# Probability times values in groups B and C: P's transpose as the stationary operand, values streaming

## The chip, the cores and the metric

The kernel runs on one core of a Trainium2 chip. The metric is device microseconds of one execution; less is better. The engines are TensorE (PE in the profile; its weight loads stand apart as PEld), VectorE (DVE), ScalarE (ACT), GpSimd (POOL) and the DMA queues that SyncE (SP), ACT and POOL issue to. In a matmul one operand, the stationary one, is first loaded into the array (a weight load), then the other, the moving one, streams through it; the result lands in PSUM. In this kernel a product of float32 operands shows two weight loads and two matmul records in the trace, one pair per pass; a product of the rounded type float32r shows one.

## The reference

Two layers, each a mixer of four parallel head groups over 2048 latent tokens and 256 context tokens (2304 keys, 18 tiles of 128). A is grouped-query attention, D a state-space scan; neither is touched. B and C matter here:

```
# B, per head: two softmax maps over all 2304 keys, then one product with the values
p1 = softmax32(einsum('bhqd,bhtd->bhqt', q1, k1) * scale)
p2 = softmax32(einsum('bhqd,bhtd->bhqt', q2, k2) * scale)
o  = einsum('bhqt,bhtd->bhqd', p1 - lam * p2, v)      # d = 64
y  = rms_norm(o, subln_g) * (1 - lam_init)
# C, per head: 8x16 clamped neighbourhood on a 64-wide grid, plus all 256 context keys
p  = softmax32(concat([s_win + bias, s_ctx]))
o  = einsum('bhwij,bhiwjd->bhwd', p_win, v_win) + einsum('bhwt,bhtd->bhwd', p_ctx, vc)
```

Each group has 4 heads of 64 channels. Context queries (2 tiles) are computed in the first layer alone. Every output is multiplied by its gate; concatenation, output projection and layer norm follow.

## The kernel before

A layer runs D and the first projection, then a chain of ten attention units (`a0, b0, a1, b1, c0, b2, c1, b3, c2, c3`), then the output projection. A unit b or c is one head: `attend` walks over query tiles of 128 (16 latent, 2 more for context in layer 0). Within the chain the order of the instructions on PE, ACT and DVE is the order in which the code is written; outside it a scheduler orders them. Into the unit that runs, `F` (a queue of "fill" work, the next unit's projection) puts matmul triples at fixed places (`F.pe()`, lines 377 to 379, tile `pj`), with their ACT and DVE steps.

One iteration `i` of `attend` works on several query tiles at once: scores of tile i+1, softmax of tile i, transposes, copies and value products of tiles i-1 and i-2, norm or finish of tile i-2 or i-3.

- `scores` (L1001): float32r matmuls into the PSUM banks `sx`, `sy`, `sz`. `maxes` (DVE L1045, or L1039 and L1041 in C) and `exp` (ACT L1060, into SBUF tiles `Ta`, `Tb`) follow. B's second map is folded in by `combine` (DVE L1084).
- `trans` (L1100): PE transposes P by key tile of 128, four at a time, into `tr`; `evac` (ACT L1114) copies the four to SBUF as `PT` (keys on the partitions, queries along the row).
- `pv` (L1126): one product per key tile. The stationary operand is the tile of values (keys x 64 channels), the moving one `PT` (keys x 128 queries). Even key tiles write partitions 0 to 63 of `acc`, odd ones 64 to 127; so the output is channels by queries, in two partial sums, and each product uses half of the array's columns.
- `ycopy` (L1131, ACT) copies `acc` to SBUF as `ys`; `ysum` (L1137, PE) multiplies it, as stationary operand, with `fold` (two identities of 64, one below the other): this adds the halves and turns the sum to queries by channels, in a new `acc`.
- `norm` (B: ACT L1143 and L1147, two POOL steps) and `finish` (DVE L1156) read that `acc`, scale, gate, and a DMA writes the output.

B has 18 key tiles per latent query tile: four groups of 4 and one of 2. C has, for the 12 interior query tiles of a head, 7: two context tiles and four full ones, and last a half tile of 64 keys, so that this product has 64 rows; the 4 edge tiles have 6. Context queries have 2. `acc` is one PSUM bank with one buffer.

The trace names the values by the tile that holds them in the unit (`b_v`, `a_q`, `a_gt`).

Of the kernel before, what the change touches and what calls it, by code (L numbers as in the profile page):

```python
# [9 lines left out]
F32 = mybir.dt.float32  # L10
# [148 lines left out]
class Net:  # L159
# [10 lines left out]
    def consts(self):  # L170
        nc, io = self.nc, self.io
        c = self.c = self.pool(self.es, "consts")
        self.dram = self.pool(self.es, "scratch", space=bass.MemoryType.DRAM)
        self.psum = self.pool(self.es, "psum", space=bass.MemoryType.PSUM)
        jp = c.tile([128, 128], I32, name="jp")
        nc.gpsimd.iota(jp, pattern=[[1, 128]], base=0, channel_multiplier=-1)
        self.ident = c.tile([128, 128], F32, name="ident")
        nc.vector.tensor_scalar(self.ident, jp, 0.0, None, op0=OP.is_equal)
        self.mhalf = c.tile([128, 8], F32, name="mhalf")
        nc.vector.memset(self.mhalf, -0.5)  # L180
        self.one = c.tile([128, 1], F32, name="one")
        nc.vector.memset(self.one, 1.0)
        self.fold = c.tile([128, 128], F32, name="fold")
        for i in range(2):
            nc.vector.tensor_add(self.fold[:, i * 64:i * 64 + 64], self.ident[:, 0:64], self.ident[:, 64:128])
        self.half = c.tile([128, 64], F32, name="half")
        nc.vector.memset(self.half, 0.5)
        self.two = c.tile([128, 128], F32, name="two")
        nc.vector.memset(self.two, 2.0)
        self.mod = [c.tile([128, 24, 2], F32, name=f"mod{l}") for l in range(DEPTH)]  # L190
        self.bT = [c.tile([128, 24], F32, name=f"bT{l}") for l in range(DEPTH)]
        for l in range(DEPTH):
            nc.sync.dma_start(self.bT[l], io["b_ada_t"][l])
        self.coef = [c.tile([128, 2, 2, 16], F32, name=f"coef{l}") for l in range(DEPTH)]
        self.cs = c.tile([128, NK, 2], F32, name="cs")
        cc = c.tile([128, NK, 2], F32, name="cc")
        nc.sync.dma_start(cc, io["cc"])
        th = c.tile([128, NK, 2], F32, name="th")
        nc.scalar.activation(th, cc, AF.Tanh, scale=0.5)
        nc.vector.scalar_tensor_tensor(self.cs, th, 1.0, cc, op0=OP.add, op1=OP.mult)  # L200
        nc.vector.tensor_scalar(self.cs, self.cs, 0.5, None, op0=OP.mult)
        dr = self.dram
        self.hs = {(l, t): dr.tile([128, 2, NK, 128], F32, name=f"hs{l}_{t}") for l in range(DEPTH) for t in range(NT)}
        self.x1 = {t: dr.tile([128, D], F32, name=f"x1_{t}") for t in range(NT)}
        self.dg = {t: dr.tile([128, 256], F32, name=f"dg_{t}") for t in range(NT)}
        self.y = {(l, t): dr.tile([128, D], F32, name=f"y{l}_{t}")
                  for l in range(DEPTH) for t in range(NT if l == 0 else NLAT)}
# [746 lines left out]
    def attend(self, l, G, F):  # L954
# [161 lines left out]
        def pv(t, g):  # L1116
            grp, g0, nkt = group(t, g)
            if not grp:
                return
            if g == 0:  # L1120
                acc[t] = self.ps_acc(128)
            PT = R[t, 0].pop(("PT", g))
            for j, (kt, c, w) in enumerate(grp):
                x = g0 + j
                half = 0 if x == nkt - 1 and nkt % 2 else x % 2
                nc.tensor.matmul(acc[t][half * 64:half * 64 + 64, :], G["v"][:w, kt, :], PT[:w, j, :], start=(x < 2),  # L1126
                                 stop=x >= nkt - 2)

        def ycopy(t):
            ys = R[t, 0]["ys"] = p.tile([128, 128], F32, name="ys")  # L1130
            nc.scalar.activation(ys, acc.pop(t), AF.Copy)  # L1131

        def ysum(t):

            r = R[t, 0]
            y = self.ps_acc(128)
            nc.tensor.matmul(y, r["ys"], self.fold, start=True, stop=True)  # L1137
            r["y"] = y[:, 0:64]

        def norm(t):  # L1140
            r = R[t, 0]
# [17 lines left out]
        def at(i, f, *a):  # L1159
            if 0 <= i < n:  # L1160
                f(steps[i], *a)
# [19 lines left out]
        for i in range(n + (3 if maps == 2 else 2)):  # L1181
            if maps == 2:
                at(i - 2, pv, 1)
                F.act()
                at(i, maxes, 0)
                at(i, neg_max, 0)
                at(i - 1, sums, 1)
                at(i - 1, recip, 1)
                at(i - 1, factor)
                at(i, exp, 0, 0)  # L1190
                at(i, scores, 1, 0)
                at(i - 1, combine, 0)
                at(i, exp, 0, 1)
                F.pe(1)
                at(i, scores, 1, 1)
                F.pe(1)
                if not early:
                    at(i - 2, trans, 2)
                at(i - 2, evac, 2)
                at(i - 2, trans, 3)  # L1200
                at(i, exp, 0, 2)
                at(i - 2, evac, 3)
                at(i, scores, 1, 2)
                at(i - 2, pv, 2)
                at(i - 2, trans, 4)
                F.dve()
                F.pe(1)
                at(i - 3, finish)
                at(i, maxes, 1)
                at(i - 2, pv, 3)  # L1210
                F.act()
                F.pe(1)
                F.pe()
                F.act()
                early = i < n and not F.merged
                at(i - 2, evac, 4)
                F.act()
                if early:
                    at(i - 1, trans, 0)
                at(i - 2, pv, 4)  # L1220
                yield half()
                at(i, sums, 0)
                at(i, neg_max, 1)
                at(i, recip, 0)
                at(i, exp, 1, 0)
                at(i, exp, 1, 1)
                if not early:
                    at(i - 1, trans, 0)
                at(i + 1, scores, 0, 0)
                F.pe()  # L1230
                at(i - 1, evac, 0)
                F.act()
                at(i + 1, scores, 0, 1)
                at(i - 1, trans, 1)
                at(i - 1, combine, 1)
                at(i - 2, ycopy)
                at(i, exp, 1, 2)
                at(i - 2, ysum)
                at(i - 1, evac, 1)
                at(i + 1, scores, 0, 2)  # L1240
                prep_at(i + 4, prep_q)
                F.pe(1)
                at(i - 2, norm)
                if i % 2:
                    F.keys()
                F.act()
                prep_at(i + 2)
                F.pe(2)
                if i % 2 == 0:
                    F.keys(1)  # L1250
                    F.keys_copy()
                F.keys_copy()
                at(i - 1, pv, 0)
                early = i + 1 < n and not F.merged
                F.dve()
                if early:
                    at(i - 1, trans, 2)
            else:
                if i == 0:
                    at(0, maxes, 0)  # L1260
                    at(0, neg_max, 0)
                    at(1, scores, 0)
                F.pe()
                at(i + 1, maxes, 0)
                at(i - 1, trans, 0)
                at(i - 1, trans, 1)
                at(i, exp, 0, 0)
                at(i - 2, ycopy)
                at(i - 1, sums, 0)
                at(i - 2, ysum)  # L1270
                at(i, exp, 0, 1)
                at(i - 1, evac, 0)
                F.pe(2)
                F.dve()
                at(i - 1, evac, 1)
                prep_at(i + 3)
                F.act()
                F.pe(1)
                at(i - 1, recip, 0)
                at(i + 1, neg_max, 0)  # L1280
                yield half()
                at(i - 2, finish)
                F.pe(1)
                prep_at(i + 5, prep_q)
                F.pe()
                F.pe(2)
                F.pe(1)
                at(i + 2, scores, 0)
                F.keys()
                F.act()  # L1290
                at(i - 1, pv, 0)
                F.dve()
                at(i - 1, pv, 1)
                F.pe(1)
                F.act()
                F.keys_copy()
            half()
            yield i < n - 1
# [705 lines left out]
```

## Time and profile before

| | |
|---|---|
| three runs | 5153.1, 5156.62 (median), 5166.4 us |
| profiled execution | 5158.76 us, its span 5156.9 us |
| mean granted TensorE clock | 0.958 of 2.4 GHz |
| PE busy | 91% of the span |
| ACT busy, DVE busy | 50%, 62% |
| units b and c | 803 to 1034, 1321 to 1530, 1550 to 2230, 3384 to 3620, 3900 to 4940 us |

A PE record begins when the instruction is issued and ends when its last result has left the array, so records of matmuls that follow each other overlap; the time that one costs the engine is the distance between starts, or between ends, in a steady row of them. A record that waits for its weights begins early and is long. The shapes in a PE record are rows by columns of the stationary operand, joined by `*`, and then those of the moving one. `<- issue` behind idle time means that the profile shows no other instruction that was waited for.

### The profile page before, as it was taken

The page shows a single profiled execution, that of the slowest core. Times are in us where ns is not written, and L with a number is a line of the kernel's source. Part 1 is how long each engine was busy: PE and PEld are TensorE (multiplying, and loading weights), DVE is VectorE, ACT ScalarE, POOL GpSimd, SP SyncE. Part 2 cuts the span into 40 slices and gives each one's busy share as a digit, 9 for nine tenths or more (in the row PEclk, how much of TensorE's full clock was granted, in tenths as well). Part 3 has the DMA queues.
Part 4 walks back from the last instruction along what each step waited for, and adds up shares of the span by engine and source line. Part 5 has one row for each costly group of instructions (what it writes and reads, how often), then busy time and mean ns, then how long its engine had stood idle before and what let it go on. Part 6 is the DMA issues. An engine that isn't in the chain of part 4 may idle for free. (4 is left out here: it accounts for less than half of the span.)

```text
span 5156.9 us, 85866 instructions
## 1 busy us (share of the span) xinstructions
PE 4681.1 (91%) x31076; PEld 3585.3 (70%) x31076; DVE 3215.5 (62%) x7061; ACT 2568.4 (50%) x6522; POOL 1912.5 (37%) x3035
## 2 busy tenths in 40 slices
PE   7788998899999999998996879988999999999998
PEld 3686646665678777776676866566657777877777
DVE  8473767676674846724972737686767648476245
ACT  3332346634675856744341233466346658566431
POOL 4363443434233233321642534434342332333112
PEclk8899999999999999999998999999999999999999
DMA  7847212322235344253668573123223343433432
GB/s 255 287 151 202 88 41 66 98 95 72 91 121 167 103 144 132 83 178 116 194 213 281 169 198 109 49 65 98 95 72 98 111 152 100 155 122 117 130 134 107
DMA packets 360184, 677.66 MB, mean 131 GB/s; under 512 B 161872, under 2 KB 262224, under 8 KB 306768
## 3 DMA queue, kind: packets, MB, share of 16 engines
q0 software_dynamic: 54432, 396.39, 22.9%
q1 hardware_dynamic: 299280, 270.47, 17.9%
q10 hardware_dynamic: 6048, 5.31, 0.3%
q8 instruction: 247, 4.05, 0.3%
q14 instruction: 177, 1.45, 0.1%
HBM read 561.66 MB, written 110.36 MB: 130 GB/s over the span
## 5 line engine op out<-in xcount | busy, mean ns | idle before, releaser
L377 PE MATMUL pj<-WH,hs 128*128 128x256 f32 (+2 forms) x2592 | 814.9, 314 | 22.1 <-ACT b_v L733 7.1
L378 PE MATMUL pj<-WL,hs 128*128 128x256 f32 (+2 forms) x2592 | 753.3, 291 | 2.7 <-POOL WL L367 2.7
L379 PE MATMUL pj<-WH,hs 128*128 128x256 f32 (+2 forms) x2592 | 752.3, 290 | 0.0
L1114 ACT ACTIVATE PT<-tr 128x512 f32<-128x512 f32 (+1 forms) x788 | 440.5, 559 | 310.0 <-PE tr L1100 303.3
L377 PEld LDWEIGHTS pj<-WH,hs 128*128 128x128 f32 x2592 | 498.1, 192 | 125.3 <-issue 68.2
L388 POOL DMA_DIRECT2D hs<-hs x378 | 227.7, 603 | 956.0 <-PE pj L379 475.6
L378 PEld LDWEIGHTS pj<-WL,hs 128*128 128x128 f32 x2592 | 499.2, 193 | 26.6 <-POOL WL L367 3.3
L881 ACT ACTIVATE PT<-sx 128x512 f32<-128x512 f32 x584 | 315.3, 592 | 378.1 <-PE sx L879 367.6
L379 PEld LDWEIGHTS pj<-WH,hs 128*128 128x128 f32 x2592 | 497.7, 192 | 2.4 <-issue 2.4
L1045 DVE TENSOR_REDUCE sm<-sx 128x1 f32<-128x1024 f32 (+1 forms) x276 | 321.8, 1166 | 210.2 <-PE sx L1001 208.9
L1060 ACT ACTIVATE Ta<-sx,sm 128x1024 f32<-128x1024 f32 (+1 forms) x340 | 324.5, 955 | 108.2 <-DVE sm L1054 87.2
L886 PE MATMUL acc<-PT,a_v 128*64 128x512 f32 (+1 forms) x1168 | 315.8, 617 | 0.0
L897 POOL TENSOR_TENSOR Ta<-Ta,PT 128x512 f32<-128x512 f32 x160 | 219.5, 1389 | 204.4 <-ACT PT L881 203.9
L1126 PE MATMUL acc<-PT,b_v 128*64 128x128 f32 (+1 forms) x3200 | 277.9, 290 | 4.4 <-DVE sm L1073 1.5
L1001 PE MATMUL sx<-b_kst,qs 128*128 128x512 f32 (+2 forms) x618 | 218.3, 441 | 58.1 <-ACT Ta L1060 57.4
L814 DVE TENSOR_REDUCE mxa<-sy 128x1 f32<-128x1024 f32 (+1 forms) x256 | 209.8, 820 | 89.9 <-PE sy L812 86.8
L897 DVE TENSOR_TENSOR Ta<-Ta,PT 128x512 f32<-128x512 f32 x288 | 217.0, 794 | 77.0 <-ACT PT L881 76.5
L878 PE MATMUL sx<-Tb,a_kst 128*128 128x512 f32 x584 | 246.8, 423 | 19.5 <-ACT PT L881 19.5
L1100 PE MATMUL tr<-ident,Ta 128*128 128x128 f32 x1576 | 246.5, 278 | 13.9 <-ACT PT L1114 10.2
L1045 DVE TENSOR_REDUCE sm<-sy 128x1 f32<-128x768 f32 (+1 forms) x260 | 245.4, 944 | 15.7 <-PE sy L1001 14.4
L814 DVE TENSOR_REDUCE mxa<-sz 128x1 f32<-128x512 f32 x256 | 175.5, 686 | 123.5 <-PE sz L812 121.7
L377 PE MATMUL s<-WH,hs 128*128 128x256 f32 (+1 forms) x576 | 193.4, 337 | 44.9 <-DMA hs<-hs 20.7
(388 smaller groups left out, 12175.2 us busy)
## 6 DMA issues: line engine op xcount, KB each, us to landing
hs<-hs POOLq DMA_DIRECT2D x378, 1024.0 KB, 5.2
hs<-hs SPq DMA_DIRECT2D x36, 1024.0 KB, 4.8
hs<-in_w_ada SPq DMA_DIRECT2D x48, 512.0 KB, 4.5
wst<-in_w_in SPq DMA_DIRECT2D x576, 32.0 KB, 1.9
yin<-y SPq DMA_DIRECT2D x30, 512.0 KB, 4.0
h<-in_xT SPq DMA_DIRECT2D x18, 512.0 KB, 6.6
U<-ud SPq DMA_DIRECT2D x64, 144.0 KB, 3.6
x<-zn SPq DMA_DIRECT2D x18, 512.0 KB, 2.7
```

Of the source, the lines that this page charges most:

```text
L377: nc.tensor.matmul(ps, H[:, k, :], WH[k][:, c0:c1], start=(k == 0), stop=False)
L378: nc.tensor.matmul(ps, H[:, k, :], WL[k][:, c0:c1], start=False, stop=False)
L379: nc.tensor.matmul(ps, L[:, k, :], WH[k][:, c0:c1], start=False, stop=(k == NK - 1))
L814: nc.vector.tensor_reduce(nm if one else mx[:, j:j + 1], s, axis=AX.X, op=OP.max, negate=one)
L878: nc.tensor.matmul(o[:, h * 512:h * 512 + w], kst[:, ks], Q[0][:, h, :w], start=True, stop=False)
L881: nc.scalar.activation(PTs[x][h][:, :w], o[:, h * 512:h * 512 + w], AF.Exp, scale=0.125)
L886: nc.tensor.matmul(acc[h * 64:(h + 1) * 64, :w], v[:, kts[x], :], PT[h][:, :w], start=(x == 0), stop=(x == n - 1))
L897: eng.tensor_tensor(sums[e][:, h, :w], first[:, :w], PT[h][:, :w], op=OP.add)
L1045: nc.vector.tensor_reduce(mx[:, j:j + 1] if len(tiles) > 1 else nm, s, axis=AX.X, op=OP.max, negate=len(tiles) == 1)
L1060: nc.scalar.activation(r["P"](a, b), src, AF.Exp, bias=r["sm"][:, 5:6], accum_out=r["sm"][:, 6 + j:7 + j])
L1114: nc.scalar.activation(PT[:w, x:y], tr[:w, x * 128:y * 128].rearrange("p (a b) -> p a b", b=128), AF.Copy)
L1126: nc.tensor.matmul(acc[t][half * 64:half * 64 + 64, :], G["v"][:w, kt, :], PT[:w, j, :], start=(x < 2), stop=x >= nkt - 2)
```

## The change

`pv` swaps the operands: the stationary one is `PT` (keys x 128 queries), the moving one the values (keys x 64 channels). All key tiles add up in one `acc` of 128 queries x 64 channels, in order. That is already what `norm` and `finish` read, so `ycopy`, `ysum` and the constant `fold` (two DVE additions at the start) go. The value products of group A (L886) stay as they were.

```diff
             if g == 0:
-                acc[t] = self.ps_acc(128)
+                acc[t] = self.ps_acc(64)
             PT = R[t, 0].pop(("PT", g))
             for j, (kt, c, w) in enumerate(grp):
                 x = g0 + j
-                half = 0 if x == nkt - 1 and nkt % 2 else x % 2
-                nc.tensor.matmul(acc[t][half * 64:half * 64 + 64, :], G["v"][:w, kt, :], PT[:w, j, :], start=(x < 2),
-                                 stop=x >= nkt - 2)
-
-        def ycopy(t):
-            ys = R[t, 0]["ys"] = p.tile([128, 128], F32, name="ys")
-            nc.scalar.activation(ys, acc.pop(t), AF.Copy)
-
-        def ysum(t):
-
-            r = R[t, 0]
-            y = self.ps_acc(128)
-            nc.tensor.matmul(y, r["ys"], self.fold, start=True, stop=True)
-            r["y"] = y[:, 0:64]
+                nc.tensor.matmul(acc[t], PT[:w, j, :], G["v"][:w, kt, :], start=(x == 0), stop=(x == nkt - 1))
+            if g0 + len(grp) == nkt:
+                R[t, 0]["y"] = acc.pop(t)
...
                 at(i - 1, combine, 1)
-                at(i - 2, ycopy)
                 at(i, exp, 1, 2)
-                at(i - 2, ysum)
                 at(i - 1, evac, 1)
...
                 at(i, exp, 0, 0)
-                at(i - 2, ycopy)
                 at(i - 1, sums, 0)
-                at(i - 2, ysum)
                 at(i, exp, 0, 1)
```

In the chain nothing else moves on PE, ACT and DVE. Between the layers (output projection of layer 0, D and first projection of layer 1) the scheduler puts some 1,100 of PE's instructions at other places, by at most 57.

PE before, inside an iteration of b0: the product of the last group of two key tiles, scores, fill, transposes, fold. Rows are PE's instructions in order, with output tile, operands, output shape (partitions x columns) and count; `pj` is fill work.

```order
L1126 MATMUL acc<-PT,b_v 64x128 x2
L1001 MATMUL sx<-b_kst,qs 128x512 x2
L377 MATMUL pj<-WH_6952,hs 128x384
L378 MATMUL pj<-WL_6954,hs 128x384
L379 MATMUL pj<-WH_6952,hs 128x384
L1001 MATMUL sz<-b_kst,qs 128x512
L1100 MATMUL tr<-ident,Ta 128x128 x4
L1137 MATMUL acc<-fold,ys 128x128
L1001 MATMUL sy<-b_kst,qs 128x512
```

The same place now; lines have moved up by 3 or 4.

```order
L1122 MATMUL acc<-b_v,PT 128x64 x2
L998 MATMUL sx<-b_kst,qs 128x512 x2
L374 MATMUL pj<-WH_6949,hs 128x384
L375 MATMUL pj<-WL_6951,hs 128x384
L376 MATMUL pj<-WH_6949,hs 128x384
L998 MATMUL sz<-b_kst,qs 128x512
L1097 MATMUL tr<-ident,Ta 128x128 x4
L998 MATMUL sy<-b_kst,qs 128x512
```

The value products have the operands and the output shape swapped and stand where they stood; the fold is gone, and the scores into `sy` follow the transposes.

ACT before, in the same iteration: exponentials, copies of transposes, and the copy of `acc` between them.

```order
L1114 ACTIVATE PT<-tr 128x512
L1131 ACTIVATE ys<-acc 128x128
L1060 ACTIVATE Tb,sm_8328<-sy,sm_8328 128x768
L1114 ACTIVATE PT<-tr 128x512
L1143 ACTIVATE yy<-acc,sm_7889 128x64
```

ACT now:

```order
L1111 ACTIVATE PT<-tr 128x512
L1057 ACTIVATE Tb,sm_8313<-sy,sm_8313 128x768
L1111 ACTIVATE PT<-tr 128x512
L1129 ACTIVATE yy<-acc,sm_7886 128x64
```

The copy is gone and the exponential moves up to its place; `yy` reads the sum of the value products directly.

## Rows read from the trace of the kernel before

**Rows 1.** The page's part 1: engines, busy us (share of the span), instructions.

```profile
PE 4681.1 (91%) x31076; PEld 3585.3 (70%) x31076; DVE 3215.5 (62%) x7061; ACT 2568.4 (50%) x6522; POOL 1912.5 (37%) x3035
```

**Rows 2.** Busy time by stretch; the sum is over five stretches of groups B and C.

```profile
837.00:849.32 12.32, 12.16 (x87) 9.75 (x87) 10.59 (x23) 9.52 (x27) 5.14 (x10) 1.00 0.25 88
3900.00:4940.00 1040.00, 978.45 (x7891) 809.10 (x7890) 609.38 (x1442) 672.78 (x1813) 308.37 (x619) 0.96 0.39 122
sum 2396.00, PE 2240.07 PEld 1839.59 DVE 1534.88 ACT 1597.07 POOL 799.94; mean PE 448.01 PEld 367.92 DVE 306.98 ACT 319.41 POOL 159.99
...
2417.00:3050.00 633.00, 531.22 (x3163) 450.27 (x3164) 412.01 (x954) 200.49 (x440) 275.39 (x321) 0.92 0.68 213
```

**Rows 3.** Instructions on tile acc: count, duration ns min/median/max, start of first and last.

```profile
L1126 PE MATMUL acc<-PT,b_v x3200: 269/273/477, 809.3 to 4934.4; 128*64 128x128 f32 x183, 64*64 64x128 f32 x6
L1126 PE MATMUL acc<-PT,a_q x1600: 269/273/477, 1545.4 to 4749.6; 128*64 128x128 f32 x172, 64*64 64x128 f32 x6
L1137 PE MATMUL acc<-fold,ys x544: 270/275/579, 819.8 to 4935.4; 128*128 128x128 f32 x182
L1131 ACT ACTIVATE ys<-acc x272: 250/277/324, 818.2 to 4934.8; 128x128 f32<-128x128 f32 x136
```

**Rows 4.** TensorE in order of time, a B iteration: start, us, line, shapes, records.

```profile
840.82 0.34 PE L379 MATMUL pj<-WH,hs 128*128 128x384 f32 x1
841.09 0.66 PE L1126 MATMUL acc<-PT,b_v 128*64 128x128 f32 x8
841.68 0.44 PE L377 MATMUL pj<-WH,hs 128*128 128x384 f32 x1
841.96 0.34 PE L378 MATMUL pj<-WL,hs 128*128 128x384 f32 x1
842.13 0.34 PE L379 MATMUL pj<-WH,hs 128*128 128x384 f32 x1
...
842.83 0.60 PE L1100 MATMUL tr<-ident,Ta 128*128 128x128 f32 x4
843.36 0.44 PE L1126 MATMUL acc<-PT,b_v 128*64 128x128 f32 x4
843.73 0.73 PE L1001 MATMUL sx<-b_kst,qs 128*128 128x512 f32 x2
```

**Rows 5.** TensorE in order of time, float32 products with 128 stationary columns (group A).

```profile
597.65 0.40 PE L812 MATMUL sz<-a_kst,Tb 128*128 128x512 f32 x1
597.88 1.05 PE L834 MATMUL tr<-two,Ta 128*128 128x128 f32 x8
```

**Rows 6.** Weight loads of 128 columns beside 64-column matmuls (scores of group C).

```profile
1535.62 0.19 PEld L1001 LDWEIGHTS sx<-a_kst,qs 128*128 128x128 f32 x1
...
1535.74 0.19 PEld L1001 LDWEIGHTS sx<-a_kst,qs 128*128 128x128 f32 x1
```

**Rows 7.** TensorE, then its weight loads, around one C query tile (idle time in brackets).

```profile
1560.79 1.08 PE L1001 MATMUL sy<-a_kst,qs 128*128 128x512 f32 x6
1561.80 1.24 PE L1126 MATMUL acc<-PT,a_q 128*64 128x128 f32 x14
1562.97 0.39 PE L377 MATMUL pj<-WH,hs 128*128 128x256 f32 x1
1563.19 0.28 PE L378 MATMUL pj<-WL,hs 128*128 128x256 f32 x1
1563.31 0.28 PE L379 MATMUL pj<-WH,hs 128*128 128x256 f32 x1
...
1562.61 0.19 PEld L1126 LDWEIGHTS acc<-PT,a_q 64*64 64x64 f32 x2 [0.17 <-issue]
```

**Rows 8.** Who waited for whom: us in total, times, longest.

```profile
PEld acc L1126 <- issue: 111.9, 570, 1.2
PE sx L1001 <- ACT Ta L1060: 57.4, 51, 4.4
PEld tr L1100 <- ACT PT L1114: 49.2, 162, 1.9
```

More of the change, by code (lines that the diff above doesn't have):

```diff
@@ L182, in consts @@
         nc.vector.memset(self.one, 1.0)
-        self.fold = c.tile([128, 128], F32, name="fold")
-        for i in range(2):
-            nc.vector.tensor_add(self.fold[:, i * 64:i * 64 + 64], self.ident[:, 0:64], self.ident[:, 64:128])
         self.half = c.tile([128, 64], F32, name="half")
```

## Prediction

> **What bounds the kernel now.** I read the page's busy times first, then the busy time by stretch, then TensorE in order of time, and last the waits. PE is busy 91% of the span, the next engine 62% [rows 1]. One whole period of a B unit lasts 12.32 us, of which PE is busy 12.16 and ACT 9.52; over the five stretches of B and C units PE is busy 2240 of 2396 us [rows 2]. So inside these units an instruction that PE loses or gains counts nearly in full, and what ACT loses counts only where PE waits for ACT. The question is thus what a value product costs PE before and after. Its busy time can't tell (records overlap); I take distances between ends of records in a steady row.
>
> **A value product before.** The tile view counts 3200 + 1600 records of L1126, and the a_gt units have 1600 more like the a_q ones; each product has two, so 3200 products, and 544 / 2 = 272 folds, as many as copies on ACT [rows 3]. By code they are 512 groups of 4 and 128 of 2 in B, 16 of 2 for context queries, 96 groups of 7 and 32 of 6 in C: 2048 + 288 + 672 + 192 = 3200.
>
> - A group of 4: L379 before it ends at 841.16 (start plus length), L377 behind it at 842.12: 0.96 us, less the 0.17 of L377 itself (L378 to L379 start 0.17 apart), is 0.79 [rows 4].
> - A group of 2: from the end of the transposes, 843.43, to the end of two scores matmuls, 844.46, less two times 0.23 (a 512-column matmul, 597.65 to 597.88 [rows 5]): 0.57 [rows 4].
> - The difference, 0.22 for two products, is 0.11 each: two passes of 128 columns, with the two column halves of the array running side by side. The rest, 0.79 - 0.44 = 0.35 us, is paid once per group. It is a gap on the way in and one on the way out: 570 times, 111.9 us in all (0.20 each), the weight load of L1126 came after idle time that ends at nothing but "issue" [rows 8], with the first load uncovered in both directions.
> - A group of 6 is then 0.79 + 0.22 = 1.01. A group of 7 is read in C: L1001 ends at 1561.87, L377 at 1563.36, less 0.12 (L378 to L379): 1.37 [rows 7]. Its half tile of 64 rows costs 0.36 instead of 0.11, since the same gap of 0.17 stands before its load ("64*64", [rows 7]).
>
> The Trainium skill (TensorEngine Tiling (Array Packing), Key Properties) says that a change of the tiling mode drains TensorE; the gaps of [rows 7, 8] are that. By it a 64-row product among 128-row ones still drains after the change.
>
> **A value product after.** No half columns, so no gap on the way in or out for full tiles. But now 128 columns are loaded for 64 that stream. The nearest row: L834 in group A has the same type and the same 128 x 128 stationary shape, and eight passes take (1.05 - 0.27) / 7 = 0.111 us apart [rows 5]; loads that run beside 64-column matmuls start 0.11 apart as well [rows 6]. Streaming 64 float32 columns takes about half of L834's, some 0.053, and hides under the next load. So a pass costs 0.111, a product 0.222, twice what it was, and what is saved is the 0.35 per group.
>
> - Group of 4: 8 x 0.111 = 0.89 against 0.79: +0.10. x 512 = +51 us.
> - Group of 2: 0.44 against 0.57: -0.13. x 144 = -18.
> - Group of 6: 1.33 against 1.01: +0.32. x 32 = +10.
> - Group of 7: twelve full passes end their stream at 11 x 0.111 + 0.053 = 1.27; then the half tile, which I take to drain: 0.35, plus 0.05 because its first load has 128 columns instead of 64, plus 0.11 + 0.05 for two passes: 1.84 against 1.37: +0.47. x 96 = +45.
> - Folds: 272 x 2 x 0.111 = -60.
>
> Sum on PE: +28 us; of it B gives +51 - 16 - 28 = +7, C the rest. What bounds the price of a pass: streaming alone, 0.053, would give 6400 x 0.058 = 371 us less, but it is excluded by [rows 5, 6], where the load sets the distance; so the lower end is the 0.110 of the transposes, (0.60 - 0.27) / 3 [rows 4], 6 us less. The upper end is load and stream one after the other, 0.11 + 0.05 = 0.16, which gives 314 more. I take 0.111, which two different rows show.
>
> The upper end is a rule of the Trainium skill (TensorE: Matmul & The Clock Gate, The mechanism): weight loads overlap matmuls in flight only when the row group differs. [Rows 5] speak against it here: a load of 128 columns takes 0.11 [rows 6], a stream of 128 float32 columns 0.110 (the transposes, [rows 4]), and L834's passes with both stand 0.111 apart, not 0.22, with one row group. By the rule the sum would be +28 + 314.
>
> **ACT and DVE.** ACT loses 272 copies of 0.277 (75 us) and its wait for the last value product. In the B period PE is idle for 0.16 of 12.32 us, so there this is worth next to nothing. Where PE does wait, it is for exponentials before L1001 (57.4 us over the run) and, as weight load, for copies before L1100 (49.2) [rows 8]; the copy stood ahead of both kinds on ACT. Bounds: 0 and -70 (two thirds of their sum, since the copy precedes one exponential and one copy per iteration, not all). I take -6, near the end that the B period shows. The two DVE additions for `fold` lie at the start beside DMA: 0. `acc` is freed by `norm` or `finish`, as before, and earlier. No wait is added: a group's first load waited for `PT` before as well.
>
> **Between the layers** (2417 to 3050, PE busy 531 of 633 us [rows 2]) the scheduler shuffles instructions by at most 57 places; nothing in the rows prices that. I take 0, bounds -15 and +15 (2.4% of the stretch).
>
> Sum: +28 - 6 = +22 on the profiled execution's 5158.8: 5181. The median of the runs is 2 us lower: 5179; I say 5180.
>
> **Rivals.**
>
> 1. The half tile doesn't drain. For it: the 64-wide transposes of the same half tile (L1100) run on without a gap; against it: the 0.17 of [rows 7] before a product whose rows alone had changed. Then a group of 7 costs 14 x 0.111 = 1.55, +0.18 instead of +0.47: 28 us less, 5152. Chance 0.15.
> 2. Faster: ACT sets the end. If in C, where ACT's copy waits for value products, the 70 us of PE's waits for exponentials and copies go, the result is 5158.8 + 28 - 70 - 2 = 5115. It decides from a relief of 44 us on (then below 5141). For it: C is where most of these waits lie; against: C's iterations are full of PE work too. Chance 0.09.
> 3. The granted clock falls. It was 0.96 in the last B and C stretch and 1.00 in the B period [rows 2]; the array now streams half as long in a value product, but also no longer stands in the gaps. If it lost 0.03 over the 2396 us, that is +72: 5252. Chance 0.08.
> 4. Loads don't hide: 5180 + 314 = 5494. Chance 0.03.
>
> **How the numbers follow.** The forecast, passes at about 0.111 and the half tile draining, has 0.60, with a range of its own from 5158 to 5205 (a pass between 0.109 and 0.114, relief 0 to 20, shuffle +-10); the 0.05 that is left is the shuffle alone or something unseen. A change of 0.3% (15.5 us: below 5141, above 5172) is about what can be told from none. Slower: three quarters of the forecast (0.45), rivals 3 and 4 (0.11), 0.01 of the rest: 0.57. Same: a quarter of the forecast (0.15), rival 1 (0.15), and 0.03: 0.33. Faster: rival 2 and a little of the rest: 0.10. The range for 8 in 10 takes in the forecast and rival 1, and part of 3: 5140 to 5225.
>
> **What the profile after would show.** Loads of `acc<-v,PT` with 128 columns, 0.11 apart in a group; no idle "issue" time before them except at the 64-row ones; between L376 and L374 around a group of 4, 0.89 us instead of 0.79; a B period of 12.32 + 4 x 0.10 - 0.13 - 0.22 = 12.37 us. Loads 0.16 apart show rival 4, no gap at "64*128" rival 1, a B period with a clock under 1.00 rival 3. If C's unfilled iterations at the end of layer 1 got shorter, my reading that PE sets their length is wrong.

## The result and the profile after

The changed kernel takes 5238.6 us (median of 4 runs, 5237.0 to 5239.7) against 5157.3 of the kernel before on the same chip: 1.0155 times as long, 95% interval [1.0137, 1.0173], or 81 us slower. The forecast was 5180, its range ended at 5225. The profiled execution's span grew from 5156.9 to 5237.9 us, so the traces show the whole of it.

The page of the changed kernel, part 1, answers to [rows 1]: busy us, share of the span, instructions.

```profile
PE 4770.7 (91%) x30532; PEld 3923.5 (75%) x30532; DVE 3213.6 (61%) x7059; ACT 2513.4 (48%) x6250; POOL 1906.5 (36%) x3035
```

PE has 544 records fewer (the folds) and is busy 90 us longer; ACT lost its 272 copies and 55 us. So the loss shows on PE. Whether it is the forecast's terms is read from the same places as before. TensorE of the changed kernel in order of time, in a B iteration like that of [rows 4]:

```profile
834.62 0.34 PE L376 MATMUL pj<-WH,hs 128*128 128x384 f32 x1
834.79 1.00 PE L1122 MATMUL acc<-b_v,PT 128*128 128x64 f32 x8
835.60 0.42 PE L374 MATMUL pj<-WH,hs 128*128 128x384 f32 x1
```

From 834.96 to 836.02 are 1.06 us, less the 0.17 of L374 itself: 0.89, as forecast, against 0.79. A C query tile of the changed kernel answers to [rows 7]:

```profile
1578.93 0.60 PE L685 MATMUL tr<-ident,ks 128*128 128x128 f32 x4
1579.37 1.81 PE L1122 MATMUL acc<-a_q,PT 128*128 128x64 f32 x14
1581.11 0.38 PE L374 MATMUL pj<-WH,hs 128*128 128x256 f32 x1
```

From 1579.53 to 1581.49, less 0.12: 1.84, again the forecast's figure (1.37 before). Loads of 128 columns hide, 0.112 apart. The gap at the entry and exit of the column-tiled mode (value products that each use half of the array's columns) is gone: in place of the 111.9 us of [rows 8], no weight load of L1122 comes after idle time that ends at "issue". That holds for the 64-row product too, where the forecast wanted to see such a gap as the sign of a drain. It shows in the starts of the loads instead: the first of the two below starts 0.26 us behind the load ahead of it (1580.48), and L374's load 0.25 behind the second (1581.11).

```profile
1580.74 0.18 PEld L1122 LDWEIGHTS acc<-a_q,PT 64*128 64x128 f32 x1
1580.85 0.19 PEld L1122 LDWEIGHTS acc<-a_q,PT 64*128 64x128 f32 x1
```

So the price of a product was right, and the loss of 81 us is three times the +28 that the forecast adds up for PE. Where the rest lies shows when the tiles are followed by the end of each tile's `yo` (written in L1142, in the kernel before L1156), worked out from the two traces:

- **Inside the units.** Ten tiles of the second B unit take 111.4 us before and 113.9 after, +0.25 a tile; the forecast's terms for B make +0.05 (4 x 0.10 - 0.13 - 0.22). In the first B unit of each layer nothing changed (-0.5 and -0.2 us over the unit without its last two tiles): there PE waits for ACT, and the longer products fill that wait. C tiles grew by 0.26, as forecast.
- **At the ends of units.** The last two tiles of the four B units of layer 1, where the projection work that fills PE has run out, took 26.6, 27.0, 20.6 and 24.6 us before and 8.3, 2.9, 4.6 and 5.2 more after: 21 us that the forecast doesn't have. In layer 0, where the last two tiles are the short context tiles, they took 2.5, 1.6, 1.6 and 3.0 us less.

The stretches of those ten tiles, before and after: busy us of PE, PEld, DVE, ACT and POOL with their counts, granted clock, DMA share, GB/s.

```profile
1374.73:1486.10 111.37, 111.37 (x931) 90.20 (x930) 97.30 (x175) 95.67 (x241) 28.71 (x55) 1.00 0.29 98
```

```profile
1368.24:1482.10 113.86, 113.50 (x912) 107.89 (x912) 96.91 (x175) 94.07 (x231) 28.82 (x55) 1.00 0.29 96
```

The clock is full in both, so here it is not rival 3; but PE, which had no idle time at all by this view, now has some. TensorE in order of time shows where it stands. First the kernel before, from a tile's transposes to the next queries' transposes:

```profile
1426.16 0.60 PE L1100 MATMUL tr<-ident,Ta 128*128 128x128 f32 x4
1426.60 0.39 PE L1137 MATMUL acc<-fold,ys 128*128 128x128 f32 x2
1426.74 0.60 PE L1001 MATMUL sy<-b_kst,qs 128*128 128x512 f32 x2
1427.17 0.28 PE L377 MATMUL pj<-WH,hs 128*128 128x256 f32 x1
1427.29 0.28 PE L378 MATMUL pj<-WL,hs 128*128 128x256 f32 x1
1427.41 0.28 PE L379 MATMUL pj<-WH,hs 128*128 128x256 f32 x1
1427.54 0.63 PE L989 MATMUL tr<-ident,qn 128*128 128x128 f32 x4
```

And the changed kernel at the same place of a later iteration, then a row of its weight loads there:

```profile
1443.64 0.60 PE L1097 MATMUL tr<-ident,Ta 128*128 128x128 f32 x4
1443.99 0.59 PE L998 MATMUL sy<-b_kst,qs 128*128 128x512 f32 x2
1444.43 0.28 PE L374 MATMUL pj<-WH,hs 128*128 128x256 f32 x1
1444.55 0.28 PE L375 MATMUL pj<-WL,hs 128*128 128x256 f32 x1
1444.67 0.28 PE L376 MATMUL pj<-WH,hs 128*128 128x256 f32 x1
1445.02 0.63 PE L986 MATMUL tr<-ident,qn 128*128 128x128 f32 x4
```

```profile
1444.99 0.42 PEld L986 LDWEIGHTS tr<-ident,qn 128*128 128x128 f32 x4 [0.25 <-issue]
```

Without the fold the queries' transposes would come 0.22 us earlier, but they follow L376 by 0.35 (1444.67 to 1445.02) instead of 0.13 (1427.41 to 1427.54). They write the bank `tr`, which ACT is still emptying for the tile's own transposes:

```profile
1444.28 0.60 ACT L1111 ACTIVATE PT<-tr 128x512 f32<-128x512 f32 x1 [0.45 <-PE tr L1097]
```

That copy ends at 1444.88, just ahead of the load at 1444.99. The list of waits counts this idle time over the run, before and after (us in total, times, longest). It grows by 11 us and is only a part of what the folds left, since these transposes come in every second tile; the dummy product below gives the rest.

```profile
PEld tr L989 <- issue: 18.0, 28, 2.0
```

```profile
PEld tr L986 <- issue: 29.4, 65, 2.0
```

The ends of units differ in another way: the granted clock. The same three tiles at the end of the fourth B unit of layer 1, before and after:

```profile
4711.40:4754.40 43.00, 35.10 (x268) 27.74 (x266) 15.77 (x35) 19.35 (x56) 17.41 (x36) 0.88 0.33 95
```

```profile
4781.20:4829.40 48.20, 40.12 (x252) 36.68 (x251) 15.53 (x36) 18.21 (x51) 18.39 (x36) 0.75 0.27 82
```

In both, PE sits idle for 3.3 us in front of L747 (now L744), waiting for DVE, and the clock goes to 1.2 GHz:

```profile
PE tr L747 <- DVE ks L741: 3.3, 1, 3.3
```

```profile
PE tr L744 <- DVE ks L738: 3.3, 1, 3.3
```

The clock comes back 10.2 us later before, 23.9 after. Added up from the traces' clock records from 800 us on, half-clock time went from 307 to 392 us. At the ends of the four B units of layer 1 the stretches grew from 23.9, 13.7, 6.8 and 10.2 us to 44.4, 20.5, 20.5 and 23.9.

So the theory to test: of 81 us, some 30 are the products as forecast, the folds' price was in B not gained but turned into waits for the copy out of `tr`, and some 30 are a clock that stays low longer at the units' ends. The rival for the ends: longer products delay a chain of dependent work there, whatever the clock.

### The profile page after: what moved, and what is told of

Read it like the earlier page. It is cut to its first block, busy times and chain, and to the rows that moved or that the text cites. A ratio compares the mean times of both kernels' runs of the same rounds, so it can differ in the third digit from the quotient of the medians.

```text
span 5237.9 us, 84521 instructions
## 1 busy us (share of the span) xinstructions
PE 4770.7 (91%) x30532; PEld 3923.5 (75%) x30532; DVE 3213.6 (61%) x7059; ACT 2513.4 (48%) x6250; POOL 1906.5 (36%) x3035
## 5 line engine op out<-in xcount | busy, mean ns | idle before, releaser
L374 PE MATMUL pj<-WH,hs 128*128 128x256 f32 (+2 forms) x2592 | 813.3, 314 | 21.5 <-ACT b_v L730 7.2
L376 PE MATMUL pj<-WH,hs 128*128 128x256 f32 (+2 forms) x2592 | 755.4, 291 | 0.0
L374 PEld LDWEIGHTS pj<-WH,hs 128*128 128x128 f32 x2592 | 502.4, 194 | 93.1 <-issue 39.1
L376 PEld LDWEIGHTS pj<-WH,hs 128*128 128x128 f32 x2592 | 501.2, 193 | 2.2 <-issue 2.2
L1122 PE MATMUL acc<-b_v,PT 128*128 128x64 f32 (+1 forms) x3200 | 426.5, 278 | 3.4 <-ACT PT L1111 3.0
L1122 PEld LDWEIGHTS acc<-b_v,PT 128*128 128x128 f32 (+1 forms) x3200 | 415.4, 200 | 11.9 <-ACT PT L1111 5.0
```

The lines of the kernel that those rows point to most:

```text
L374: nc.tensor.matmul(ps, H[:, k, :], WH[k][:, c0:c1], start=(k == 0), stop=False)
L376: nc.tensor.matmul(ps, L[:, k, :], WH[k][:, c0:c1], start=False, stop=(k == NK - 1))
L1122: nc.tensor.matmul(acc[t], PT[:w, j, :], G["v"][:w, kt, :], start=(x == 0), stop=(x == nkt - 1))
```

## Experiments

Ratios are to the kernel before on the same chip, each with its 95% interval; "worth" is the difference of such ratios times 5157 us. Unit and tile times come from the profiled execution.

### All products stream twice

```
-                nc.tensor.matmul(acc[t], PT[:w, j, :], G["v"][:w, kt, :], ...)
+                nc.tensor.matmul(acc[t].rearrange("p (a d) -> p a d", a=2), PT[:w, j, :],
+                                 G["v"][:w, kt, None, :].to_broadcast([w, 2, 64]), ...)
```

> The changed kernel, but each value product streams its 64 value columns twice (128 columns into a 128-wide accumulator, of which the first half is used). Theory (clock): some 35 of the 82 us that were lost are stretches at half the granted clock that last longer behind the units' ends, because the array streams for only half of each 0.112 us pass; with 128 columns the pass stays at 0.11 (the load sets it), the half-clock time falls from 511 us back towards 434, and the kernel takes about 5205 us. Rival 1 (latency: the longer value products themselves delay the units' ends): half-clock time stays near 511 and the time at 5239 +-6. Rival 2 (load and stream add up): passes grow to 0.16 and the time to over 5400.

Measured: 1.0136 [1.0122, 1.0150], 5238.0 us. By the time alone the rival won. The trace says otherwise: half-clock time from 800 us on fell from 392 to 291 us, and the last two tiles of the four B units came 10.5, 7.3, 8.0 and 6.6 us sooner than in the changed kernel (32 in all). What it gained there it paid elsewhere: passes inside a group stayed 0.112 apart, but a group of 4 ahead of transposes lasts 0.05 longer and a group of 7 0.11, so most units grew by 1 to 3 us. The start of the first layer and that of the second B unit of layer 1 took some 5 us longer each, where the other runs spread from 824 to 832 us and from 312 to 318. An edit that touches every product can't settle it by time; the next one touches few.

### Only the last four tiles of a B unit stream twice

```
+        tail = steps[-4:] if maps == 2 else []
...
+                if t in tail:
+                    (the doubled product above, into 128 columns)
+                else:
                     nc.tensor.matmul(acc[t], PT[:w, j, :], G["v"][:w, kt, :], ...)
```

> The changed kernel, but only the value products of the last four tiles of every B unit stream their 64 value columns twice; all others are as in the changed kernel. Theory (clock at the units' ends): the half-clock stretches behind the B units of layer 1 shrink as they did when all products streamed twice (there 3616:44.4 us became 13.7, 4121:20.5 and 4462:20.5 went, 4797:23.9 became 6.8, and the four units' ends came 32 us earlier), while the 1 to 1.5 us that every unit paid for the longer stream is left out: about 5239 - 32 = 5207. Rival (the ends came earlier by something else, such as a schedule shifted by the longer products of the whole unit): within 10 us of 5239.

Measured: 1.0121 [1.0106, 1.0136], 5221.9 us: worth 17 us, about half of what was expected. In the trace the four ends came 8.1, 5.9, 6.6 and 6.7 us sooner, 27 in all. The stretch of the last view, in this kernel:

```profile
4753.60:4795.10 41.50, 33.46 (x252) 30.64 (x252) 15.52 (x36) 18.32 (x51) 18.30 (x36) 0.92 0.32 95
```

The same instructions, more columns to stream, and 41.5 us instead of 48.2, at a clock of 0.92 instead of 0.75. PE's wait for DVE in it is the same 3.3 us, and so are its other waits in the list (2.1 us for the copies out of `tr`, then 0.9, 0.8 and 0.6). So it is the clock and not the chain: longer products in the same chain made it shorter. This is shown for the four ends, in one execution. That one, 5210.2 us, was the fastest of its run (the others 5220.7 to 5225.6, at a mean clock of 0.955 to 0.957 against 0.959), so the 27 us are at the high end; the median gives 17.

### The 64-row product padded to 128 rows

```
+                if w < 128:
+                    nc.gpsimd.memset(PT[w:, x:y], 0.0)
...
-                nc.tensor.matmul(acc[t], PT[:w, j, :], G["v"][:w, kt, :], ...)
+                nc.tensor.matmul(acc[t], PT[:, j, :], G["v"][:, kt, :], ...)
```

> The changed kernel, but the 64-row product of C's window tiles is made a product over 128 rows (the other 64 rows of P's transpose are zeroed by GpSimd). Theory (the 64-row tile among 128-row ones still drains, as before the change): a group of 7 falls from about 1.9 us to 14 x 0.112 = 1.57, 96 times, so about -28 us: 5211. Rival (the half tile does not drain, a group of 7 is long for another reason): 5239 +-5.

Measured: 1.0109 [1.0091, 1.0128], 5215.2 us: worth 24 us. TensorE of this kernel around a group of 7 (L1124 is L1122 there):

```profile
1947.95 1.08 PE L998 MATMUL sx<-a_kst,qs 128*128 128x512 f32 x6
1948.87 1.67 PE L1124 MATMUL acc<-b_v,PT 128*128 128x64 f32 x14
1950.35 0.36 PE L374 MATMUL pj<-WH,hs 128*128 128x256 f32 x1
```

From 1949.03 to 1950.71, less 0.12: 1.56, or 14 x 0.111. Changing the rows of the tile alone costs 0.28 us in the form without column halves too. Rival 1 of the prediction falls.

### A dummy product in the fold's place

```
+        def dummy(t):
+            r = R[t, 0]
+            nc.tensor.matmul(r["y"][:, 64:192], self.ident, self.ident, start=True, stop=True)
+            r["y"] = r["y"][:, 0:64]
...
+                at(i - 2, dummy)
```

> The changed kernel with one dummy matrix product per tile (128 columns of float32, two passes, identity by identity, its result unused) at the place where the fold stood; no copy on ScalarE. Theory (a good half of the time that the fold left is spent on waiting for ScalarE to empty the bank of the transposes, 0.17 of 0.22 us per B tile): the dummy costs about 30 us, 5269. Rival (all of the fold's time was gained, and the loss lies elsewhere): 272 x 0.222 = 60 us, 5299.

Measured: 1.0220 [1.0207, 1.0233], 5275.4 us: worth -34, near the 30 expected, far from 60. The traces split it more sharply than I did: ten tiles of the second B unit take 114.1 us with the dummy and 113.9 without, 0.02 a tile for 0.22 us of work; a C tile of the units with fill takes 0.22 longer (three full ones: 20.8 and 21.5 us), the full price. In `c3`, the unit without fill, the dummy costs 0.22 and nothing in turn; its tiles had grown by 0.26 and 0.44 in turn. All C units together take 21 us longer with it, of 30 (136 x 0.222). TensorE of this kernel in the second B unit:

```profile
1451.57 0.39 PE L1128 MATMUL acc<-ident 128*128 128x128 f32 x2
1451.71 0.60 PE L998 MATMUL sy<-b_kst,qs 128*128 128x512 f32 x2
1452.15 0.28 PE L374 MATMUL pj<-WH,hs 128*128 128x256 f32 x1
1452.27 0.28 PE L375 MATMUL pj<-WL,hs 128*128 128x256 f32 x1
1452.39 0.28 PE L376 MATMUL pj<-WH,hs 128*128 128x256 f32 x1
1452.52 0.63 PE L986 MATMUL tr<-ident,qn 128*128 128x128 f32 x4
```

The gap ahead of L986 is back to 0.13. In this stretch the queries' transposes start 0.14 us behind the end of ACT's copy out of `tr` in all three kernels, the one before, the changed one and this one: the copy sets the time, with or without a product ahead of it. Over the ten tiles, told by the ends of records, the 2.23 us of the dummies reappear without them as 1.13 us ahead of the queries' transposes, 0.55 ahead of the keys' (L744) and 0.44 ahead of scores in `sy`. In B the fold stood in a wait; taking it out gave nothing.

### One part alone

```
+        new = maps == 2          # the other kernel: maps == 1
...
+            if new:              # product of the changed kernel, y = acc
...
+            if new:              # in the copy and in the fold
+                return
```

> The kernel before with the new form of the value products in B units alone; C units keep column halves, copy and fold. By the two traces (unit by unit, end of each unit's last tile) B units lost 47 us of the 81 and C units 35: 5157 + 47 = 5204, and the half-clock stretches behind the B units of layer 1 stay long. Rival (the forecast's terms: B +7, C the rest): 5164.

> The kernel before with the new form of the value products in C units alone; B units keep column halves, copy and fold. The new form in B alone cost 49 us, so if the two parts add up, C alone costs 82 - 49 = 33: 5190. The half-clock stretches behind the B units of layer 1 should be as short as before. Rival 1 (the forecast's terms for C, +28 - 7 = 21 us): 5178. Rival 2 (the stretches at half clock come from C's products too): over 5205, with the stretches as long as with both.

Measured: B alone 1.0092 [1.0074, 1.0110], 5210.0 us, worth -47; C alone 1.0069 [1.0055, 1.0084], 5191.0 us, worth -36. The sum, 83, is the whole loss. The forecast's terms for C, 21, lie just outside its interval (28 to 43). The low clock at the ends goes with B: the last two tiles of the four B units of layer 1 took 20 us longer than before with B changed and 4 us less with C changed. The same three tiles as above, first B alone, then C alone:

```profile
4765.70:4813.70 48.00, 39.91 (x251) 36.46 (x250) 15.47 (x35) 18.17 (x51) 18.29 (x36) 0.75 0.27 82
```

```profile
4749.60:4791.30 41.70, 33.70 (x269) 26.62 (x267) 15.60 (x35) 19.38 (x56) 18.33 (x36) 0.92 0.33 96
```

### Fewer entries into the column-tiled mode

If the column-tiled mode costs its 0.35 us per entry and exit, it is the rows of products that should be longer. Three merges per B tile, in the kernel before and in the changed one:

```
+                if early:
+                    at(i - 1, trans, 2)
                 at(i - 1, pv, 0)
-                if early:
-                    at(i - 1, trans, 2)
...
+                at(i - 2, pv, 2)
+                at(i - 2, pv, 3)
                 at(i - 2, pv, 4)
```

> The kernel before, with the value products of a B tile issued in two rows (groups 0 and 1, then 2, 3 and 4) instead of five: three of five entries into the column-tiled mode and exits from it go, 128 x 3 = 384. Theory (0.35 us is paid once per entry and exit, whatever the row's length): 384 x 0.35 = -134 us: 5023. Rival 1 (the gap belongs to every group of four, or to the wait for P's transpose): 5157 +-10. Rival 2 (the later products make others wait, for the accumulator and the copies of P's transpose): half of it is given back, about 5090.

> The changed kernel with the same two rows of value products per B tile. Theory: nothing is paid per group, so nothing is to be had: 5239 +-10. Rival (the order itself is worth something, whatever the tiling): as much faster as the kernel before gets by it, some 60 to 130 us.

Measured: 0.9983 [0.9972, 0.9993], 5155.5 us, from the kernel before; 1.0353 [1.0339, 1.0367], 5348.6 us, from the changed one. The rivals about the gap fall, and so does my 5023: the order costs 102 us where no gap is saved (1.0353 less 1.0155), and saves 9 where gaps are, so the gaps are worth 111 of the 134 that I put on them, if the order costs both kernels the same, which isn't shown. What the order costs shows in the second B unit: ten tiles' transposes out of `Tb` end 3.2 us later in sum, waiting for the copy out of `tr`, which value products no longer cover.

> The kernel before with two of five entries into the column-tiled mode per B tile taken away (groups 0 and 1 in one row, 3 and 4 in one row), but group 2 left between the two transposes where it covers ScalarE's copy. With three merges PE saved 4.5 us per 10 tiles in the products and gave 3.2 back waiting for that copy. Theory: 256 x 0.35 = -90 us less some 20 of waits: about 5085. Rival (every merge is paid back in waits): 5157 +-10.

Group 0 moves behind the transposes of group 2 as above; groups 3 and 4:

```
-                at(i - 2, pv, 3)
...
-                if early:
-                    at(i - 1, trans, 0)
+                at(i - 2, pv, 3)
                 at(i - 2, pv, 4)
+                if early:
+                    at(i - 1, trans, 0)
```

Measured: 0.9949 [0.9937, 0.9961], 5134.6 us, worth 26 of the 70 expected. Per ten tiles scores in `sy` lost 2.3 us and transposes out of `Ta` 1.5. The next one leaves those transposes ahead:

> As the version with two merges of the kernel before (groups 0 and 1, and 3 and 4 of a B tile in one row each), but the next tile's first transposes stay ahead of groups 3 and 4, where they were; with them behind, scores waited 0.23 us per tile and transposes 0.15. Theory (those waits come from that move alone): 5135 - 128 x 0.38 = about 5087. Rival (any order that delays group 3 gives its gap back elsewhere): 5135 +-10.

```
-                at(i - 2, pv, 3)
...
                 if early:
                     at(i - 1, trans, 0)
+                at(i - 2, pv, 3)
                 at(i - 2, pv, 4)
```

Measured: 0.9914 [0.9901, 0.9927], 5115.3 us, 18 better than the last, not 48. Ten tiles fell from 111.4 to 107.8 us, and this is the trace of it, with a row of 12 and one of 16 records:

```profile
1430.53 0.60 PE L1100 MATMUL tr<-ident,Ta 128*128 128x128 f32 x4
1431.06 0.88 PE L1126 MATMUL acc<-PT,b_v 128*64 128x128 f32 x12
1431.87 0.73 PE L1001 MATMUL sx<-b_kst,qs 128*128 128x512 f32 x2
...
1435.42 0.28 PE L379 MATMUL pj<-WH,hs 128*128 128x256 f32 x1
1435.54 0.60 PE L1100 MATMUL tr<-ident,Tb 128*128 128x128 f32 x4
1436.07 1.09 PE L1126 MATMUL acc<-PT,b_v 128*64 128x128 f32 x16
```

A row of 12 records (6 products) lasts 0.22 longer than one of 8 in [rows 4]: two products at 0.11, and no second gap. The row of 16 is 0.21 longer than that of 12.

> As the version before it, and C's 64-row product padded to 128 rows by a GpSimd memset, as in the padded version of the changed kernel, where that gave 24 us. Theory (the 64-row tile drains in the column-tiled form as well, 0.36 against 0.11 us): 96 x 0.25 = -24 us beside the two merges, about 5063. Rival (in the column-tiled form the last, odd product is late for another reason): no difference between the two.

> The kernel before with two merges per B tile and C's 64-row product padded, as in the last version, but group 1 is drawn up to group 0, ahead of the transposes of group 2, instead of those transposes being put ahead of group 0. Where these stood ahead, the first of them came 0.31 us behind the projection's last product in a full row and 0.11 where nothing was waited for: they waited for ScalarE to empty their bank. Theory (the products of groups 0 and 1 now cover that copy): 5108 - 128 x 0.2 = about 5082. Rival (group 1's own copy isn't done by then and PE waits for it instead): 5108 +-10.

The padding is the memset of the padded version above; group 1 is moved so:

```
                 at(i - 1, pv, 0)
+                at(i - 1, pv, 1)
                 early = i + 1 < n and not F.merged
...
-                at(i - 2, pv, 1)
```

Measured: 0.9903 [0.9888, 0.9918], 5107.7 us, with the padding; 0.9903 [0.9885, 0.9921], 5109.9 us, with group 1 drawn up to group 0 besides. By the ratios the padding is worth 6 us of the 24 expected, which the intervals don't tell from nothing; in the trace it took 0.15 us from a C tile (0.25 expected). So the rival holds in part: padded, a group of 7 still takes 0.21 longer than one of 6, and not 0.11. In the trace of the kernel before, records of two products start in pairs, 0.007 us apart, a new pair every 0.10; the seventh product has no partner, and its two records end 0.11 apart. That this is the reason was not tested. The other order took 0.08 more from a B tile (107.0 us per ten) and lost it in the medians. Both are faster than the kernel before and the changed one by about 50 and 130 us, and not told apart.

## Why the prediction was wrong

- **The price of a product** was right within 0.01: 0.89 for a group of 4, 1.84 for a group of 7, loads hidden at 0.112 (between projection products the median group of 4 grew by 0.11, not 0.10). So were the gap of the column-tiled mode, paid once per row, and the drain of the half tile after the change, 0.28 measured by padding against the forecast's 0.29. Before the change only 0.15 of its 0.36 us went with the padding.
- **The folds, "272 x 2 x 0.111 = -60"**, is the step that failed first. It rests on "an instruction that PE loses or gains counts nearly in full", read from PE's busy share. In C that held where there is fill (the dummy costs a C tile 0.22). In B it didn't: the dummy costs a tile 0.02. So of 60 us about half was gained (the dummies put back cost 34, in the traces mostly in C), and the 28 of B's latent tiles turned into waits, most of them for ACT's copy out of `tr`. I had priced ACT's relief, but not looked at whether ACT's copy would be late for the next writer of its bank once PE came sooner.
- **The granted clock** had no term in the sum. Rival 3 named it with a chance of 0.08 and put it everywhere (0.03 over the 2396 us, +72). In the B period the clock stayed 1.00, so the sign that I gave for it didn't show; it fell at the ends of the units, after idle time of 3.3 us that was there before as well. The traces of the runs that streamed twice put 27 us (last four tiles) and 32 (all tiles) on four such ends; by its median the former gained 17.
- **The sum made again**, from the ends of tiles in the two traces: the B units without their last two tiles +32, their ends in layer 1 +21, in layer 0 -9, C +35, all the rest +2, which is 81 us. The forecast has +7 for all of B, +21 for C and -6 for ACT's relief. That its +28, with 28 for B's folds and 27 for the ends, makes 83 as well is partly chance: this leaves out the ends of layer 0, the first B units, which hide their share (some 10 us) in PE's waits for ACT, and what C lost beyond its terms. ACT's relief and the stretch between the layers (+7 in the changed trace, between -5 and +13 in the others, which have the same code there) can't be told from the differences between executions.
- **B +7** measured +47, and C +21 measured +36. B's difference is the two steps above. In the traces C's units grew by 2 to 5 us each, but `c1` of layer 0 by 10: one tile there took 8.9 us instead of 3.0, with PE waiting 2.3 us for DVE ahead of L685 and a granted clock of 0.53 over the 10 us behind it. With C alone changed this unit grew by 8 us, with the doubled tails by 2, though the C code is the same; why is open.
- **Rival 2** (ACT sets the end) does not appear: the unfilled C iterations at the end of layer 1 grew, as the forecast's last test wanted: from 39.7 to 43.2 us over eleven tiles.

## What to carry to other kernels

An engine that is busy all the time by its records can still stand in short waits for a bank or a copy; before an instruction is taken out, look at which bank the instructions behind it write and when the copy out of that bank ends, because that wait can take its place. A product that streams for half of its load's time cost nothing more here while the clock was full, but behind idle time, when the clock was low, it kept it low for longer. And where a mode costs time on the way in and out, longer rows of it (here 44 us gained by two merges) were worth more than leaving the mode (81 us lost).

## What was not expected of the hardware

After the same 3.3 us of idle TensorE, the granted clock of the stretch around it was 0.75 with products that load 128 columns and stream 64, and 0.92 with the same products streaming 128, at the same distance of 0.112 us between loads while the clock is full. And a doubled stream is free inside a row, but not always at its end: transposes behind a group of 4 came 0.05 us later, scores and projection products did not; what stands behind a group of 7, with its 64-row product, came 0.11 later.
